# The gate's product over pairs of token blocks: seven half-size products in place of eight

## The chip, the cores and the metric

The kernel runs on one core of a Trainium2 chip. Its engines, with the names the profile gives them, are TensorE (PE, with its weight loads as PEld), VectorE (DVE), ScalarE (ACT), GpSimd (POOL) and SyncE (SP, which here issues nearly all DMAs). Each engine executes its own list of instructions in order. The metric is the device time of one execution in microseconds.

## The reference

The kernel computes one decoder layer for 2048 tokens of 1024 values, cut here to its last part, which the change concerns:

```
u    = rmsnorm(x, norm_mix)
proj = u @ w_in                          # 1024 -> 4096 columns, eight groups of 512
y    = [o_a, o_b]                        # group A: HGRN2, 4 heads; group B: stick-breaking attention, 8 heads
h    = x + y @ w_out                     # 1024 x 1024
pe   = rmsnorm(p @ w_ple_proj, ple_post_norm)           # 256 -> 1024
gate = sigmoid(rmsnorm(h, ple_gate_norm) @ w_ple_gate)  # 1024 x 1024
out  = rmsnorm(h + gate * pe, final_norm)
```

## The kernel before

**Precision.** Inputs are float32. Each matmul operand is split into a high and a low float16 part (`split`, L76 on ACT and L77 on VectorE; for weights L132 and L133), and each product is three matmuls: high by high, high by low, low by high. All of them are issued from one helper, so that every matmul of the profile has line L160.

**Stages.** Tokens are cut into 4 chunks of 512, and these into 4 blocks of 128, worked through from the last to the first. Eight groups of input weights times four chunks make 32 units; A units end in a chunked scan (`mix_A`, with seven levels, whose matmuls write `lps`, then `sp` and `op`), B units in attention. Mixed results go to `y_d` in device memory. Then follows the final stage: 16 blocks of 128 tokens. For each block `y_load` reads `y_d` into `yn`, splits it and has two DMA transposes (L697) write the left operand `fy`. `final_out` multiplies it by `w_out` (2 halves of 512 columns x 8 contraction blocks x 3 = 48 matmuls), adds `x` (L732) and takes the row's reciprocal root (L712, L83, L84); 12 matmuls make the embedding's projection, which is normalised by L740. `final_tr` splits `h` and transposes it (L748), and `final_gate` multiplies it by the gate's weights: another 48 matmuls of 128x512 into tiles named `np`. Then come the sigmoid (L762, ACT), the product (L763, GpSimd; VectorE in the last block), the sum (L764), the squares (L766), the reciprocal root, and L781 with the store of the output. In the last block the second half of the gate's product is cut into 384 and 128 columns.

**Order.** A scheduler orders the built program per engine from estimated times, so that the final stage's first blocks lie among the last mix units on every engine. Within this, `run` lets a stream of matmuls advance and steps the other tasks (`spawn`) when their time is due. Weights of the output and the gate projection are prepared by such tasks in the last input group: 24 pieces of 128x512, each a load into a ring of five `raw` buffers and two splits, into buffers that held the transposed input.

**Buffers.** Tiles rotate by tag: two buffers each of `sc`, `kq` and `y`, two each of `e0` and `e1` for `h`, three PSUM banks of the pool `ps_a` for the gate, the embedding and the mix levels (`lps`), three of `ps_pj` for the output projection, one each of `ps_o` and `ps_t`; `yn` alternates between two buffers.

## Time and profile before

| what | before |
|---|---|
| median of 3 runs | 1259.11 us (1258.26 to 1259.74) |
| the profiled execution | 1257.38 us |
| its span, first to last instruction | 1255.6 us |
| mean granted TensorE clock | 0.994 |
| PE busy | 1206.9 us, 96% of the span |
| DVE busy | 872.0 us, 69% |
| ACT busy | 596.8 us, 48% |
| POOL busy | 356.4 us, 28% |

The busy shares are means over the whole span and hide that stages differ: the tables of stretches below show that the end of the span is another regime than its start. Durations in the rows are those of one execution. An instruction's duration includes the fill and drain of its pipeline, so instructions that follow one another start closer together than they last. "xN" behind a row counts equal instructions that were put into one row, and its time runs from the first start to the last end.

### The profile page before, as it was taken

Reading aid. Unit: us, or ns where it says so; the run is one execution under the profiler, and the core shown is the slowest. Engines: PE = TensorE matmul, PEld = TensorE weight load, DVE = VectorE, ACT = ScalarE, POOL = GpSimd, SP = SyncE. Lnnn points to the kernel's source line nnn. Section 1 sums busy time; section 2 is a strip of 40 time slices with the busy share of each in tenths; the row PEclk is TensorE's granted clock in tenths of the full one; section 3 lists DMA queues with packets and bytes.
Section 4 is the critical chain, followed back from the end, with each engine's and each line's share of the span. In section 5 each row is a group of like instructions: output and inputs, shape, how many; then the busy total and the mean of one; then the engine's idle time right before and its main releaser. Section 6 shows DMA issues by size and latency. Waiting matters only on the chain.

```text
span 1255.6 us, 25850 instructions
## 1 busy us (share of the span) xinstructions
PE 1206.9 (96%) x9802; PEld 771.1 (61%) x9802; DVE 872.0 (69%) x1736; ACT 596.8 (48%) x1507; POOL 356.4 (28%) x472
## 2 busy tenths in 40 slices
PE   8887899999999999999999999898999999999997
PEld 7664666777766776677677766565544444444443
DVE  5779699976589995589997568998845344344233
ACT  7665544544454454464454445565534333333222
POOL 4248441114441212444112444110121211111212
PEclk9999999999999999999999999999999999999999
DMA  9896831156661046772126565357526636346211
GB/s 271 263 225 174 186 78 33 50 148 141 151 144 29 19 118 148 156 181 48 27 75 138 139 150 118 124 160 203 129 73 152 134 102 148 103 109 144 59 51 53
DMA packets 258469, 155.42 MB, mean 124 GB/s; under 512 B 181281, under 2 KB 226337, under 8 KB 258337
## 3 DMA queue, kind: packets, MB, share of 16 engines
...
## 4 chain that ended last, share of the span: by engine, by line
PE 69%; DVE 13%; DMA 9%; ACT 3%; issue 3%; POOL 2%; SPq 1%; POOLq 0%; DVEq 0%; ACTq 0%
PE pj L160 33%; PE np L160 28%; PE op L160 3%; PE lps L160 2%; DMA at_t<-wt_t 2%; DVE wl L133 2%; PE z L160 2%; DMA raw_t<-x_nat 2%; DVE e_t L621 1%; DMA raw_t<-w_in 1%; DMA raw_t<-w_out 1%; DVE kq_t L511 1%; ACT wh L132 1%; DVE e_t L626 1%; DMA at_t<-kp_t 1%
## 5 line engine op out<-in xcount | busy, mean ns | idle before, releaser
L160 PE MATMUL pj<-wh,xh 128*128 128x256 f16 x1024 | 280.3, 274 | 3.8 <-DVE ql_t L77 3.8
L160 PE MATMUL pj<-wl,xh 128*128 128x256 f16 x1024 | 280.4, 274 | 0.0
L160 PE MATMUL pj<-wh,xl 128*128 128x256 f16 x1024 | 280.3, 274 | 0.0
L160 PEld LDWEIGHTS <-xh 128*128 128x128 f16 x2048 | 200.4, 98 | 27.4 <-issue 0.3
L160 PE MATMUL pj<-xl,wh 128*128 128x512 f16 (+1 forms) x560 | 197.0, 361 | 2.2 <-DVE xl L260 1.7
L160 PE MATMUL pj<-xh,wh 128*128 128x512 f16 (+1 forms) x560 | 196.3, 361 | 1.6 <-DMA xh<-kq_t 1.6
L160 PE MATMUL pj<-xh,wl 128*128 128x512 f16 (+1 forms) x560 | 196.9, 361 | 0.0
L84 POOL TENSOR_TENSOR rs_y<-rs_v,mhalf 128x1 f32<-128x1 f32 (+2 forms) x87 | 77.4, 890 | 307.1 <-DVE rs_v L83 306.1
L160 PE MATMUL np<-wh,fy 128*128 128x512 f16 x512 | 155.6, 379 | 0.2 <-DVE e_t L732 0.2
L160 PEld LDWEIGHTS <-at_t 128*128 128x128 f16 x1688 | 99.2, 98 | 87.8 <-DMA at_t<-wt_t 16.7
L160 PEld LDWEIGHTS <-wh 128*128 128x128 f16 x1120 | 99.8, 98 | 85.8 <-issue 3.8
L160 PEld LDWEIGHTS <-fy 128*128 128x128 f16 x768 | 74.3, 98 | 87.8 <-issue 0.5
L160 PEld LDWEIGHTS <-xl 128*128 128x128 f16 x1024 | 100.6, 98 | 19.2 <-issue 4.2
L160 PE MATMUL np<-wh,at_t 128*128 128x512 f16 (+2 forms) x264 | 98.0, 373 | 0.9 <-ACT sc_t L762 0.9
L160 PE MATMUL np<-wl,at_t 128*128 128x512 f16 (+2 forms) x264 | 98.0, 373 | 0.0
L160 PE MATMUL np<-wh,wt_t 128*128 128x512 f16 (+2 forms) x264 | 97.9, 373 | 0.0
L160 PE MATMUL np<-wl,fy 128*128 128x512 f16 x256 | 97.0, 379 | 0.0
L621 DVE TENSOR_TENSOR_SCAN e_t<-e_t,reset 128x642 f32<-128x642 f32 x56 | 84.6, 1511 | 15.6 <-ACT e_t L616 15.5
L629 ACT CAST wt_t<-e_t 128x640 f16<-128x640 f32 (+1 forms) x64 | 44.7, 698 | 105.3 <-DVE e_t L626 90.4
L160 PEld LDWEIGHTS <-wl 128*128 128x128 f16 x560 | 53.6, 98 | 59.3 <-issue 2.5
L631 POOL TENSOR_TENSOR wt_t<-e_t,wt_t 128x512 f16<-128x512 f32 (+1 forms) x64 | 77.8, 1216 | 35.2 <-ACT wt_t L629 34.8
L76 ACT ACTIVATE qch_t<-kq_t 128x256 f16<-128x256 f32 x112 | 46.3, 414 | 77.8 <-DVE kq_t L511 53.3
...
## 6 DMA issues: line engine op xcount, KB each, us to landing
raw_t<-w_in SPq DMA_DIRECT2D x61, 256.0 KB, 3.6
raw_t<-x_nat SPq DMA_DIRECT2D x56, 256.0 KB, 3.7
y_d<-y_t SPq DMA_DIRECT2D x32, 256.0 KB, 2.5
...
out<-y_t SPq DMA_DIRECT2D x31, 256.0 KB, 2.1
...
```

Of the source, the lines that this page charges most:

```text
L76: nc.scalar.activation(hi, src, AF.Copy, scale=scale)
L84: nc.gpsimd.tensor_tensor(y, v, mhalf[:, 0:n], op=ALU.pow)
L132: nc.scalar.activation(self.h[:, k, :], self.r[k], AF.Copy, scale=g)
L133: nc.vector.scalar_tensor_tensor(self.l[:, k, :], self.r[k], g, self.h[:, k, :], op0=ALU.mult, op1=ALU.subtract)
L160: nc.tensor.matmul(out_, lhsT, rhs, start=start, stop=stop)
L511: nc.vector.tensor_tensor(act, act, other, op=ALU.mult)
L621: nc.vector.tensor_tensor_scan(fl(pr_), fl(f), fl(reset), 0.0, op0=ALU.mult, op1=ALU.max)
L626: nc.vector.tensor_tensor(sg[:, :, :w_], sg[:, :, :w_], pr_[:, :, :w_], op=ALU.mult)
L629: nc.scalar.copy(wt[:, :, :w_], sg[:, :, :w_])
L631: nc.gpsimd.tensor_tensor(wt[:, :, 3 * P : 3 * P + lw], sg[:, :, :lw], wt[:, :, :lw], op=ALU.subtract)
```

## The change

A pair of token blocks is treated as a 2 x 2 matrix: rows are the two blocks of 128 tokens (`a1?`, `a2?`), columns the two halves of the 1024 contracted values (`a?1`, `a?2`). The gate's weights are likewise four quarters of 512 x 512. Where the plain product needs eight products of quarters, the Winograd form of Strassen's scheme needs seven, each 4 contraction blocks x 3 = 12 matmuls of 128x512 (84 per pair in place of 96), of sums and differences of the quarters.

- Left operands (`pair_parts`): sums and differences of `h`, of which `a11`, `s2`, `s1`, `a12`, `s3`, `s4`, `a22` are each split and transposed (L817, twice 128x512 to 4 x 128 x 128). The row's factor is now applied before the split.
- Weights: the quarters `11` and `22` are prepared in the last input group (8 pieces in place of 16 for the gate), the combinations `t1` to `t4` and the quarter `21` by `gate_combined`, a task that is started when the final stage begins. For each of 4 contraction blocks it issues 4 loads into the `raw` ring (now six buffers), 8 ACT, 6 GpSimd and 3 VectorE instructions of 128x512.
- Results (`gate_pair`): seven products in sequence; VectorE adds PSUM tiles to running sums (L878), and each of the four results then takes the way of before (sigmoid, product, sum, square). The last result of the last pair has the full 512 columns.
- The gate of a pair is computed after the out and embedding products of the pair behind it; `h` of the four blocks of two pairs lives in `e`, `gs` and `fa` buffers. `yn` has one buffer. The embedding's product uses the banks `ps_o` and `ps_t`.
- A fallback that runs at run time only if a flag is set, and is not taken with these inputs, is rewritten to match; its part of the diff is left out.

```diff
+    gq = {}
+
+    def gate_tiles(names, pool, tags):
+
+        for part, tag in enumerate(tags):
+            t = pool.tile([P, KD, CH], F16, name="gq", tag=tag)
+            for i, n in enumerate(names):
+                gq[n, part] = t[:, 4 * i : 4 * i + 4, :]
+
+    def gate_plain(names):
+
+        for n in names:
+            r, c_ = int(n[0]) - 1, int(n[1]) - 1
+            for k in range(4):
+                g = gg[:, 4 * r + k : 4 * r + k + 1]
+                t = raw("gr")
+                nc.sync.dma_start(t, w_gate[c_][:, 4 * r + k, :])
+                yield 1.5
+                nc.scalar.activation(gq[n, 0][:, k, :], t, AF.Copy, scale=g)
+                nc.vector.scalar_tensor_tensor(gq[n, 1][:, k, :], t, g, gq[n, 0][:, k, :], op0=ALU.mult, op1=ALU.subtract)
+
+    def gate_combined():
+
+        for k in range(4):
+            g1, g2 = gg[:, k : k + 1], gg[:, 4 + k : 5 + k]
+            b = {}
+            for n in ("11", "12", "22", "21"):
+                r, c_ = int(n[0]) - 1, int(n[1]) - 1
+                b[n] = raw("gr")
+                nc.sync.dma_start(b[n], w_gate[c_][:, 4 * r + k, :])
+            yield 2.0
+            for n in ("11", "12", "22"):
+                nc.scalar.activation(b[n], b[n], AF.Copy, scale=g2 if n == "22" else g1)
+            nc.gpsimd.tensor_tensor(b["11"], b["12"], b["11"], op=ALU.subtract)
+            nc.gpsimd.tensor_tensor(b["12"], b["12"], b["22"], op=ALU.subtract)
+            nc.gpsimd.tensor_tensor(b["22"], b["22"], b["11"], op=ALU.subtract)
+            yield 2.0
+            nc.scalar.activation(gq["21", 0][:, k, :], b["21"], AF.Copy, scale=g2)
+            nc.vector.scalar_tensor_tensor(gq["21", 1][:, k, :], b["21"], g2, gq["21", 0][:, k, :], op0=ALU.mult, op1=ALU.subtract)
+            nc.vector.scalar_tensor_tensor(b["21"], b["21"], g2, b["22"], op0=ALU.mult, op1=ALU.subtract)
+            for n, t in (("t1", "11"), ("t3", "12"), ("t2", "22"), ("t4", "21")):
+                nc.scalar.copy(gq[n, 0][:, k, :], b[t])
+                (nc.vector if n == "t4" else nc.gpsimd).tensor_tensor(gq[n, 1][:, k, :], b[t], gq[n, 0][:, k, :], op=ALU.subtract)
+            yield 4.0
...
-        t = kv.tile([P, KD * CH], F16, name="yn", tag=f"bkv{n % 2}")
+        t = kv.tile([P, KD * CH], F16, name="yn", tag="bkv0")
...
+    def final_emb(st, ph, pl):
+
         pps = []
-        yield from nat_proj(ps_a, "a", ph, pl, 2, lambda half, k: (wph[:, k, hss[half]], wpl[:, k, hss[half]]), pps)
+        for half, (pool, tag) in enumerate(((ps_o, "o"), (ps_t, "t"))):
+            ps = pool.tile([P, CH], F32, name="np", tag=tag)
+            n = 0
+            for k in range(2):
+                for a, bb in ((ph(k), wph), (ph(k), wpl), (pl(k), wph)):
+                    mm(ps, a, bb[:, k, hss[half]], n == 0, n == 5)
+                    n += 1
+                yield
+            pps.append(ps)
...
+    def pair_parts(s1, s2, last):
+
+        if last:
+            t = [kv.tile([P, KD * CH], F16, name="lh", tag=tag).rearrange("p (q i k t) -> p q i k t", q=4, i=2, k=4) for tag in ("bkv0", "bkv2")]
+            slots = [[t[i // 4][:, i % 4, j] for j in range(2)] for i in range(7)]
+        else:
+            slots = []
+            for tag in ("wt", "at", "kp0", "kp1", "wt", "at"):
+                t = f16(tag, (P, 2, 4, P))
+                slots.append([t[:, 0], t[:, 1]])
+            slots.append([f16(tag, (P, 4, P)) for tag in ("vh", "vl")])
+        (a11, a12), (a21, a22), r1, r2 = s1["h"], s2["h"], s1["rn"], s2["rn"]
+
+        def put(src, r=None):
+            hi, lo = f16("qh"), f16("ql")
+            if r is None:
+                nc.scalar.copy(hi, src)
+                nc.vector.tensor_tensor(lo, src, hi, op=ALU.subtract)
+            else:
+                split(hi, lo, src, r)
+            dst = slots.pop(0)
+            for d, s in zip(dst, (hi, lo)):
+                nc.sync.dma_start(d, s, transpose=True)
+            return dst
+
+        lhs = {}
+        d21, g11 = f32("sc"), f32("sc")
+        nc.gpsimd.tensor_tensor(d21, a21, a22, op=ALU.add)
+        nc.scalar.activation(g11, a11, AF.Copy, scale=r1)
+        lhs["a11"] = put(a11, r1)
+        s2_ = f32("y")
+        nc.vector.scalar_tensor_tensor(s2_, d21, r2, g11, op0=ALU.mult, op1=ALU.subtract)
+        lhs["s2"] = put(s2_)
+        lhs["s1"] = put(d21, r2)
+        lhs["a12"] = put(a12, r1)
+        nc.vector.scalar_tensor_tensor(g11, a21, r2, g11, op0=ALU.mult, op1=ALU.subtract)
+        lhs["s3"] = put(g11)
+        nc.vector.scalar_tensor_tensor(s2_, a12, r1, s2_, op0=ALU.mult, op1=ALU.subtract)
+        lhs["s4"] = put(s2_)
+        lhs["a22"] = put(a22, r2)
+        return lhs
+
+    def gate_pair(sts, rows, lhs, last):
+
+        G = p2(-SH - SW)
+        bank = []
+        ss = [small("ssg2", 2, 4) for _ in range(2)]
+
+        def part(i, half, gt):
+
+            p_, h_ = sts[i]["pe"][half], sts[i]["h"][half]
+            nc.scalar.activation(gt, gt, AF.Sigmoid, scale=G)
+            (nc.vector if last else nc.gpsimd).tensor_tensor(p_, gt, p_, op=ALU.mult)
+            nc.vector.tensor_tensor(h_, h_, p_, op=ALU.add)
+            nc.scalar.activation(f16("kn"), h_, AF.Square, accum_out=ss[i][:, half : half + 1])
+
+        def end(i):
+            h, s_ = sts[i]["h"], small("ss1", 1)
+            nc.vector.tensor_tensor(s_, ss[i][:, 0:1], ss[i][:, 1:2], op=ALU.add)
+            rf = rsqrt(s_, 1, 1.0 / D, EPS)
+            for half in range(2):
+                gf = gfin[:, hss[half]]
+                if last and i:
+                    nc.gpsimd.tensor_tensor(h[half], h[half], gf, op=ALU.mult)
+                    if half:
+                        nc.scalar.activation(h[half], h[half], AF.Copy, scale=rf)
+                    else:
+                        nc.vector.tensor_scalar(h[half], h[half], rf, None, op0=ALU.mult)
+                else:
+                    nc.vector.scalar_tensor_tensor(h[half], h[half], rf, gf, op0=ALU.mult, op1=ALU.mult)
+                (nc.scalar if last and i and half else nc.sync).dma_start(out[rows[i], hss[half]], h[half])
+
+        def prod(left, n):
+
+            bank.append(pa("gate"))
+            for k in range(4):
+                wh_, wl_ = gq[n, 0][:, k, :], gq[n, 1][:, k, :]
+                (lh_, ll_) = lhs[left]
+                for i, (a, bb) in enumerate(((lh_, wh_), (lh_, wl_), (ll_, wh_))):
+                    mm(bank[-1], a[:, k, :], bb, k == 0 and i == 0, k == 3 and i == 2)
+                yield
+
+        def plus(dst, other):
+            nc.vector.tensor_tensor(dst, bank[-1], other, op=ALU.add)
+
+        yield from prod("a11", "11")
+        x1, u2 = f32("sc"), f32("sc")
+        nc.scalar.copy(x1, bank[-1])
+        yield from prod("s2", "t2")
+        plus(u2, x1)
+        yield from prod("s1", "t1")
+        u4, c22 = f32("y"), f32("y")
+        plus(u4, u2)
+        yield from prod("a12", "21")
+        plus(x1, x1)
+        part(0, 0, x1)
+        yield from prod("s3", "t3")
+        plus(c22, u4)
+        plus(u2, u2)
+        part(1, 1, c22)
+        yield from prod("s4", "22")
+        plus(u4, u4)
+        part(0, 1, u4)
+        end(0)
+        yield from prod("a22", "t4")
+        plus(u2, u2)
+        part(1, 0, u2)
+        end(1)
...
-        if g == 7 and i0 < 3 and c > 0:
-            w_new(9 + i0)
-            spawn(prepare_task(9 + i0), 0.5, 1)
-
-    for n in range(9, 12):
-        if n not in ws:
-            w_new(n)
-            for _ in prepare_task(n):
+        if g == 7 and i0 == 0:
+            w_new(9)
+            spawn(prepare_task(9), 0.5, 1)
+        if g == 7 and i0 == 1:
+            gate_tiles(("11", "22"), xpool, ("xh2", "xl2"))
+            spawn(gate_plain(("11", "22")), 0.5, 1)
+
+    drain(len(order) - 1)
+    gate_tiles(("21", "t1"), xpool, ("xh1", "xl1"))
+    gate_tiles(("t2", "t3"), xpool, ("xh0", "xl0"))
+    t4 = kv.tile([P, KD, CH], F16, name="gq", tag="bkv1")
+    gq["t4", 0], gq["t4", 1] = t4[:, 0:4, :], t4[:, 4:8, :]
+    spawn(gate_combined(), 1.0)
+    gpost, gfin, wph, wpl = late_weights()
+    tail = len(order)
...
+    for m in range(NB // 2):
+        for n in (2 * m, 2 * m + 1):
+            run(out_block(n), tail)
+            if m:
+                run(emb_block(n - 2), tail)
+        if m == 1:
+            drain(tail)
+        final = m == NB // 2 - 1
+        if final:
+            lhs[m] = pair_parts(sts[2 * m], sts[2 * m + 1], True)
+        if m:
+            j = 2 * m - 2
+            run(gate_pair([sts[j], sts[j + 1]], [rws[j], rws[j + 1]], lhs[m - 1], False), tail)
+        if not final:
+            lhs[m] = pair_parts(sts[2 * m], sts[2 * m + 1], False)
+    j = NB - 2
+    for n in (j, j + 1):
+        run(emb_block(n), tail)
+    run(gate_pair([sts[j], sts[j + 1]], [rws[j], rws[j + 1]], lhs[j // 2], True), tail)
```

The scheduler's order of GpSimd in the last mix A unit, before: the mix's mask product (L488) and clears, and reciprocal roots (L84). Here `sc_t` and `kp_t` are the mix's tiles.

```order
L488 TENSOR_TENSOR sc_t<-kq_t 128x512
L84 TENSOR_TENSOR rs_y<-rs_v,mhalf 128x4
L84 TENSOR_TENSOR rs_y<-rs_v,mhalf 128x1
L519 MEMSET sc_t 128x512
L487 MEMSET kp_t 128x1024
L84 TENSOR_TENSOR rs_y<-rs_v,mhalf 128x1
L84 TENSOR_TENSOR rs_y<-rs_v,mhalf 128x4
```

The same place after (L530, L561 and L529 are the former L488, L519 and L487; `raw_t` holds raw weights, `gq` the float16 parts of a combination):

```order
L530 TENSOR_TENSOR sc_t<-kq_t 128x512
L84 TENSOR_TENSOR rs_y<-rs_v,mhalf 128x4
L173 TENSOR_TENSOR raw_t<-raw_t 128x512
L174 TENSOR_TENSOR raw_t<-raw_t 128x512
L182 TENSOR_TENSOR gq<-raw_t,gq 128x512
L175 TENSOR_TENSOR raw_t<-raw_t 128x512
L182 TENSOR_TENSOR gq<-raw_t,gq 128x512
L561 MEMSET sc_t 128x512
L182 TENSOR_TENSOR gq<-raw_t,gq 128x512
L529 MEMSET kp_t 128x1024
L173 TENSOR_TENSOR raw_t<-raw_t 128x512
L84 TENSOR_TENSOR rs_y<-rs_v,mhalf 128x1
```

The six instructions of the first contraction block stand around the clear of the last mix unit's tile; 18 more of the same kinds follow, mixed with reciprocal roots, and then the addition L822 of the first pair's left operands.

SyncE's queue at the same place, before: loads of the last weights and of `x`, the store of a mix result (`y_d`), transposes.

```order
L808 DMA gw<-g_post 128x1024
L809 DMA gw<-g_fin 128x1024
L788 DMA raw_t<-p_t 128x512
L726 DMA raw_t<-x_nat 128x512 x6
L377 DMA y_d<-y_t 128x4x128
L697 DMA_TRANSPOSE fy<-yn 128x8x128 x2
L726 DMA raw_t<-x_nat 128x512
L689 DMA yn<-y_d 128x1024
```

After (L956, L957, L768, L419, L739, L596 and L731 are the former L808, L809, L726, L377, L697, L554 and L689):

```order
L956 DMA gw<-g_post 128x1024
L957 DMA gw<-g_fin 128x1024
L169 DMA raw_t<-w_gate 128x512
L419 DMA y_d<-y_t 128x4x128
L169 DMA raw_t<-w_gate 128x512 x4
L739 DMA_TRANSPOSE fy<-yn 128x8x128
L596 DMA_TRANSPOSE at_t<-kp_t 128x8x128
L169 DMA raw_t<-w_gate 128x512 x3
L739 DMA_TRANSPOSE fy<-yn 128x8x128
L768 DMA raw_t<-x_nat 128x512 x2
L731 DMA yn<-y_d 128x1024
L169 DMA raw_t<-w_gate 128x512 x3
```

The loads of the gate's weights stand between the store of `y_d`, the transposes and the `x` loads; the last of the first contraction block's four is behind the store.

## Rows read from the trace of the kernel before

**Rows 1.** Stretches: us, busy (x) of PE, PEld, DVE, ACT, POOL, PEclk, DMA share, GB/s.
```profile
850.00:900.00 50.00, 45.49 (x372) 25.95 (x370) 44.00 (x106) 26.02 (x73) 3.46 (x5) 1.00 0.65 177
900.00:950.00 50.00, 49.06 (x291) 23.88 (x290) 30.18 (x71) 20.39 (x60) 11.20 (x13) 1.00 0.44 102
950.00:1000.00 50.00, 50.00 (x233) 22.68 (x232) 21.28 (x47) 18.59 (x45) 10.65 (x13) 1.00 0.58 128
```

**Rows 2.** The chain that ended last: start us, us, what.
```profile
932.93 312.28 PE np L160 x1452
```

**Rows 3.** What TensorE waited for, 780 to 960: us in total, times, longest.
```profile
PE lps L160 <- ACT kp_t L76: 6.3, 4, 2.7
PE lps L160 <- DVE qcl_t L77: 2.4, 2, 1.4
```

**Rows 4.** Weight splits in group 7: ns min/median/max, first and last start.
```profile
L133 DVE SCALAR_TENSOR_TENSOR wl<-raw_t,gg,wh x16: 739/743/745, 809.3 to 847.7; 128x512 f16<-128x512 f32 x16
```

**Rows 5.** Timeline of the end: start us, us, engine, line, out<-in, idle before.
```profile
1246.32 0.22 PE L160 MATMUL np<-wh,wt_t 128*128 128x128 f16 x1
...
1246.58 0.37 ACT L762 ACTIVATE sc_t<-np,rs_y 128x128 f32<-128x128 f32 x1 [0.70 <-PE np L160]
1246.98 0.29 DVE L763 TENSOR_TENSOR kq_t<-sc_t,kq_t 128x128 f32<-128x128 f32 x1
...
1247.30 0.29 DVE L764 TENSOR_TENSOR e_t<-e_t,kq_t 128x128 f32<-128x128 f32 x1
...
1247.80 0.31 ACT L766 ACTIVATE kn_t<-e_t 128x128 f16<-128x128 f32 x1
```

**Rows 6.** ACT by form, 858 to 1256: xcount, busy us, mean ns, idle before.
```profile
L762 ACT ACTIVATE sc_t<-np,rs_y 128x512 f32<-128x512 f32 x31 | 21.2, 685 | 72.7 <-PE np L160 72.7
...
L766 ACT ACTIVATE kn_t<-e_t 128x512 f16<-128x512 f32 x31 | 19.5, 629 | 56.8 <-DVE e_t L764 56.4 <-DVE ss L718 0.4
```

**Rows 7.** Timeline of VectorE as the final stage begins.
```profile
862.81 1.89 DVE L77 SCALAR_TENSOR_TENSOR wp<-raw_t,wp 128x512 f16<-128x512 f32 x3
...
877.31 0.42 DVE L77 SCALAR_TENSOR_TENSOR kp_t<-kq_t,kp_t 128x256 f16<-128x256 f32 x1
...
918.83 1.26 DVE L77 SCALAR_TENSOR_TENSOR sl<-st__12449,sh 128x128 f16<-128x128 f32 x1 [0.72 <-ACT sh L76]
...
922.50 0.29 DVE L77 SCALAR_TENSOR_TENSOR sl<-st__12449,sh 128x128 f16<-128x128 f32 x1 [1.43 <-ACT sh L76]
...
940.58 1.73 DVE L77 SCALAR_TENSOR_TENSOR gs_t<-e_t,fa_t 128x512 f16<-128x512 f32 x1 [0.75 <-ACT fa_t L76]
...
955.25 1.41 DVE L740 SCALAR_TENSOR_TENSOR kq_t<-np,rs_y,gw 128x512 f32<-128x512 f32 x2 [0.73 <-POOL rs_y L84]
```

**Rows 8.** Timeline of SyncE's queue.
```profile
872.72 0.40 SPq L377 DMA_DIRECT2D y_d<-y_t  x1
...
881.01 1.24 SPq L554 DMA_TRANSPOSE at_t<-kp_t  x1
```

**Rows 9.** DMA issues: count, KB each, median us from issue to landing.
```profile
raw_t<-w_gate SPq DMA_DIRECT2D x16, 256.0 KB, 3.2
...
fy<-yn SPq DMA_TRANSPOSE x32, 3.3
```

**Rows 10.** Timeline of GpSimd.
```profile
918.67 1.27 POOL L763 TENSOR_TENSOR kq_t<-sc_t,kq_t 128x512 f32<-128x512 f32 x1 [3.98 <-ACT sc_t L762]
...
940.49 1.27 POOL L763 TENSOR_TENSOR kq_t<-sc_t,kq_t 128x512 f32<-128x512 f32 x1
...
955.18 1.27 POOL L763 TENSOR_TENSOR kq_t<-sc_t,kq_t 128x512 f32<-128x512 f32 x1
```

**Rows 11.** GpSimd by form, whole span: xcount, busy us, mean ns, idle before.
```profile
L763 POOL TENSOR_TENSOR kq_t<-sc_t,kq_t 128x512 f32<-128x512 f32 x30 | 37.9, 1264 | 127.0 <-ACT sc_t L762 127.0
...
L488 POOL TENSOR_TENSOR sc_t<-kq_t 128x512 f32<-128x512 f32 x16 | 25.8, 1611 | 89.8 <-DVE kq_t L412 89.2 <-DVE rs_v L83 0.6
```

**Rows 12.** One stretch of 10 us: columns as in Rows 1.
```profile
920.00:930.00 10.00, 10.00 (x58) 4.88 (x56) 2.97 (x10) 2.95 (x10) 1.81 (x2) 1.00 0.14 28
```

More of the change, by code (lines that the diff above doesn't have):

```diff
@@ L150, in w_new @@
         else:
[L151 to L154 removed]
+            ws[n] = Weights(w_out[1], gy, xpool, (f"xh{NC - 1}", f"xl{NC - 1}"))
     clock = [0.0]
@@ L719, in row_rsqrt, with final_out @@
         return rsqrt(s_, 1, scale, eps, post)
-    def final_out(st, yh, yl, ph, pl, rows):
+    def final_out(st, yh, yl, rows, tags=("e0", "e1")):
         xn = []
@@ L773, in final_gate @@
             ot = f32("y")
-            if last:
-                nc.gpsimd.tensor_tensor(h[half], h[half], gfin[:, hss[half]], op=ALU.mult)
-            if last and half:
-                nc.scalar.activation(ot, h[half], AF.Copy, scale=rf)
-            elif last:
-                nc.vector.tensor_scalar(ot, h[half], rf, None, op0=ALU.mult)
-            else:
-                nc.vector.scalar_tensor_tensor(ot, h[half], rf, gfin[:, hss[half]], op0=ALU.mult, op1=ALU.mult)
-            (nc.scalar if last and half else nc.sync).dma_start(out[rows, hss[half]], ot)
+            nc.vector.scalar_tensor_tensor(ot, h[half], rf, gfin[:, hss[half]], op0=ALU.mult, op1=ALU.mult)
+            nc.sync.dma_start(out[rows, hss[half]], ot)
     def p_parts(src, w):
@@ L865, in trunk_kernel @@
-    run(final_gate(*prev, last=True), -1)
-    def final_block(yh, yl, ph, pl, rows):
-        st = {}
-        for _ in final_out(st, yh, yl, ph, pl, rows):
-            pass
+        if g == 7 and i0 == 0:
[6 more added lines that the diff above has]
+    gate_tiles(("21", "t1"), xpool, ("xh1", "xl1"))
@@ L871, in final_block @@
+    j = NB - 2
+    for n in (j, j + 1):
+        run(emb_block(n), tail)
+    run(gate_pair([sts[j], sts[j + 1]], [rws[j], rws[j + 1]], lhs[j // 2], True), tail)
+    def final_block(yh, yl, ph, pl, rows):
+        st = {"post": p2(-SH - SW)}
+        for stage in (lambda: final_out(st, yh, yl, rows), lambda: final_emb(st, ph, pl)):
+            for _ in stage():
+                pass
         final_tr(st)
@@ L884, in trunk_kernel, with full_rows @@
     far = nc.values_load(fint[0:1, 0:1], min_val=0, max_val=1)
-    def full_rows(rs, gkv, gyt, cc, bb):
+    def full_rows(rs, gkv, cc, bb):
         r0 = cc * CH + bb * P
         rows = bass.ds(r0, P)
-        yh, yl = gyt[:, :, 0:P], gyt[:, :, P : 2 * P]
-        ya = f32("sc")
-        nc.sync.dma_start(ya, y_d[rows, 0 : 4 * P])
-        yp = [f16(f"kp{i}") for i in range(2)]
-        split(yp[0], yp[1], ya, p2(SY))
-        for t, p_ in zip((yh, yl), yp):
-            nc.sync.dma_start(t[:, 0:4, :], p_, transpose=True)
         nc.vector.memset(rs, 0.0)
@@ L958, in trunk_kernel @@
             with tc.For_i(0, CB, 1) as bb:
-                full_rows(rs, gkv, gyt, cc, bb)
+                full_rows(rs, gkv, cc, bb)
+        for i, tags in enumerate((("xh2", "xl2"), ("xh1", "xl1"))):
+            ws[10 + i] = Weights(w_gate[i], gg, xpool, tags)
+            ws[10 + i].prepare(range(KD))
+        with tc.For_i(0, NC, 1) as cc:
+            with tc.For_i(0, CB, 1) as bb:
+                full_out(cc, bb)
 def lay_out(x, p, norm_mix, w_in, a_out_norm, b_out_norm, w_out, lb_logits,
```

92 lines of the change are left out of this document (43 added, 49 removed).

## The prediction

> **What bounds the kernel now.** I first read the table of stretches. From 950 to 1000 us TensorE is busy for all 50.00 us at full clock, and VectorE for 21.28 [rows 1]; the four rows after it, to 1200, are alike (233 or 234 matmuls each). In that steady part time is simply a count of matmuls: 233 of 128x512 in 50.00 us, so 0.2146 us each. The chain of waits says the same of the end: 312.28 us of nothing but the line of matmuls, from 932.93 on [rows 2]. The start-up of the final stage is different: in 850 to 900 VectorE is busy for 44.00 of 50 us and TensorE for 45.49 [rows 1], and the list of what TensorE waits for names the scaled halves of the last mix A units' operands, 6.3 us for ACT's `kp_t` and 2.4 us for VectorE's `qcl_t` [rows 3]. So there are two questions: how many matmuls go, and what the change puts into a start-up in which VectorE is already nearly full.
>
> **What goes: matmuls.** A pair of blocks had 2 × 48 gate products of 128x512 and gets 7 products × 4 contraction blocks × 3 halves = 84. Eight pairs save 8 × 12 = 96 matmuls, at 0.2146 us [rows 1] 20.6 us, all of it in a stretch where TensorE is the bound. In the steady part I expect nothing to take it back. A pair took 216 matmuls, 46.4 us, and takes 204, 43.8 us. VectorE gets seven adds, three combinations and three low halves more per pair, 13 × 0.6 = 7.9 us (the 0.6 is worked out below); with 21.28 of 50 [rows 1], 19.7 of 46.4, it comes to some 27 of 43.8 us. The left operands of a pair are made a whole product stage ahead.
>
> **What goes: weight splits.** Eight of the 24 splits in the last input group are not made there: 8 VectorE instructions of 0.74 us [rows 4] (and 8 casts on ACT), 5.9 us on each, in a stretch where TensorE's two largest waits come to 8.7 us [rows 3]. Most of these waits are on the mix's own chain, so I take −1 us, bounds 0 and −2.
>
> **What comes: a longer tail.** Before, the last product is cut so that only 128 columns follow the last matmul at 1246.32: sigmoid at 1246.58, product 1246.98, sum 1247.30, square 1247.80 [rows 5]; the span ends at 1255.6, 9.1 us after the last matmul's end. Now 512 columns follow. An add to the running sum comes ahead of the sigmoid (0.69 us, as any 128x512 VectorE instruction [rows 7]); the sigmoid goes from 0.37 to 0.69 and the square from 0.31 to 0.63, the means of their full-width forms [rows 6], product and sum from 0.29 to 0.69 each. That is 0.69 + 0.32 + 0.32 + 0.40 + 0.40 = 2.1 us; I take 2.2, as two output multiplications of block 14 now stand on VectorE ahead of block 15's sum. Bounds: +1.2 (only the add and the two VectorE widths not overlapped, less a shorter gap) and +3.5 (both multiplications, 1.4, in full).
>
> **What comes: the weights' combinations, as the final stage begins.** For each of four k there are 4 loads of raw weights, 8 ACT, 6 GpSimd and 3 VectorE instructions of 128x512, and the second product (s2 by t2) needs all four. GpSimd, which is idle there now but for one-column powers and clears, gets 24 of these, and one addition for the first left operand: 25.
>
> When does it begin? The queues are in order. The last of the first k's loads stands on SP behind the store of `y_d`, which is issued at 872.72 [rows 8]; a weight load lands 3.2 us after its issue [rows 9], so about 875 to 876 us on the clock of before (I take 875), and the last mix A unit is then still running.
>
> What does it cost? In the changed order VectorE has, from that point to s2's low half, 86 instructions: 30 of 128x512 with two SBUF inputs, 8 of the same with a gain column, 12 of 256 and 4 of 128 columns, and 32 that read at most one SBUF tensor (six of 512 columns from PSUM, one masked copy of 512 and eight of 256, eight of 128, nine tiny). The rows give 0.60 us for one of the first kind when they follow one another (three in 1.89), 0.42 for 256 columns with its end, 0.34 without it [rows 7], 0.74 for the gain kind, 0.70 spaced [rows 4]: 30 × 0.605 + 8 × 0.70 + 12 × 0.336 + 4 × 0.24 = 28.7 us, and the 32 others, at the same rates, 9.7 us. Alone that would be 38.4 us, to 913.
>
> But GpSimd and VectorE get in each other's way. At 918.67 GpSimd begins a product of 1.27 us, and a 128x128 subtraction that VectorE begins at 918.83 takes 1.26 us, where the same one takes 0.29 at 922.50. At 940.49 and 940.58 it happens again: 1.73 us for a 128x512 subtraction that takes 0.69 elsewhere. At 955.18 GpSimd runs the same product and VectorE's two multiplications of a PSUM tile take 1.41 together, undisturbed [rows 7, 10]. So an instruction with two SBUF inputs waits for most of GpSimd's one; from 918.67 to about 919.8 are 1.1 us. It goes both ways: GpSimd's mask product L488, made while VectorE is busy, has a mean of 1611 ns against 1264 of the gate's [rows 11].
>
> The Trainium skill, "SBUF — State Buffer", section "Who interferes with whom", states that a VectorE instruction with two SBUF inputs contends with a GpSimd instruction that reads SBUF, that one with at most one SBUF input does not, and that the later one waits for the whole of the other. The trace agrees in all three cases (1.26, 1.73 and 1.41 us). By it the 25 instructions and VectorE's 54 two-input ones would stand in one line; without it they would overlap, which is the first rival.
>
> I take the exclusive sum: 28.7 + 25 × 1.1 = 56.2 us, and half of the 9.7 of others, which can run while GpSimd holds: 61 us. From 875 that is 936. Then s2's low part has to be transposed: SP needs 1.24 us for one transpose [rows 8] and it lands 3.3 after issue [rows 9], and there is about 1.5 us of queueing behind the transposes of other operands: the second product starts at T = 942. Below that the cost could be nearly nothing (first rival), above it loads and transposes can add (second rival). What makes this bite is TensorE's own order: the last mix A levels stand at 77, 98, 119, 134 and 159 matmuls of the final stage instead of 106 to 180, and the second gate product at 216, so it can't run ahead; the other 1416 matmuls are all behind s2.
>
> **The sum.** From T: 1416 × 0.2146 = 303.9 us; some 14 small matmuls of the mix, 0.8; the tail 9.1 + 2.2 = 11.3. The span is T + 316.0. With T = 942: 1258.0. Plus 1.5 us for the projections of pair 2's first block, whose `e` buffers wait for pair 0's outputs (before, only two blocks share them; bounds 0 and 4), less 1 for the last group: 1258.5, against 1255.6 before, +2.9. The profiled execution took 1257.38, so 1260.3; it lies 1.7 under the median of the runs, 1259.11, and on that basis I predict 1262. The saving of 20.6 us is thus spent: 2.2 in the tail and about 20 in the start-up. The turning point is T near 939.6 (1255.6 − 316.0), before the two small terms.
>
> **Rivals.**
> 1. The combinations fall into gaps (faster). GpSimd has almost nothing there, and VectorE is not full everywhere: from 920 to 930 it is busy for 2.97 of 10 us [rows 12]. If the two hide under one another, GpSimd sets the pace: 875 + 2 for ACT's scalings + 25 × 1.27 = 909; three waits for the next k's raw buffers of 3.3 us make 919, VectorE's subtraction and the transpose 6: T = 925, with a little left of the collisions 927. The span is 927 + 316 + 0.5 = 1243.5, so about 1247 on the runs' basis. It decides from T below 939: each collision that is hidden is worth 1.1 us, and three of 25 are enough for a gain. For it speaks that a VectorE row that waits for a combination anyway loses nothing to a collision; against it that VectorE was at 44.00 of 50 in 850 to 900 [rows 1], before anything was added.
> 2. Data waits on top of the collisions (slower). The raw ring has six buffers and each k needs four, shared with the `x_nat` and `p` loads; in SP's order the gate's loads stand between transposes of `fy` and those of the mix, so one that waits for a buffer holds up the transposes behind it, and a VectorE row waiting for its combination holds up the mix levels behind it. At 3.3 us of landing and one transpose of 1.24 for each of three changes of k, 13.5 us: T = 955.5, the span 1272, and 1275 on the runs' basis. For it: in before's last mix A units TensorE already waits for such rows [rows 3]. Against: part of that wait is the same time in which collisions are paid.
> 3. The steady part takes its toll. Three banks rotate through the seven products, and a product can't start until the add of the third last has run; if VectorE is late by 2 us once in each of seven pairs, 14 us go, also without trouble in the start-up: 1247 + 14 = 1261. Against it: VectorE at 27 of 43.8 us a pair, and a product lasts 2.6 us against 0.7 for an add. I give it little and count it with the forecast's upper half.
>
> **How the numbers follow.** Chances: the forecast 0.50, with a range of its own of 1255 to 1271 (T from 935 to 951); rival 1 0.33; rival 2 0.14; rival 3 0.03. A measurement of this kernel tells about 0.2% from no change, 2.5 us, so "same" is 1256.6 to 1261.6. Of the forecast's 0.50 I put 0.03 below that, 0.20 in it and 0.27 above. Faster is 0.33 + 0.03 less 0.01 = 0.35; same 0.20; slower 0.27 + 0.14 + 0.03 and the rounding 0.01 = 0.45. The range takes in rival 1 from 1244 and rival 2 up to 1275.
>
> **What would show it.** Matmuls of the final stage: 1632 at 0.2146 us, packed without gaps from the second product on, and 20.6 us less of them. GpSimd's 24 combinations with durations well above 1.27 us, or VectorE's neighbours at 1.3 to 1.7 instead of 0.6, bear out the collisions; if both are at their plain durations, rival 1 holds. The first matmul of the second product near 942 bears out the sum, near 927 rival 1, near 955 rival 2; then TensorE's waits should name `wt_t` or the combined weights, and SP's waits the raw buffers. Last matmul to the end of the span: 11.3 us instead of 9.1. The forecast is wrong if the second product begins before 937, or if TensorE waits in the steady part.

## The result and the profile after

The changed kernel takes 1302.65 us (median of 4 runs, 1300.84 to 1308.58) against 1258.68: ratio 1.0358, 95% interval 1.0336 to 1.0380. It is slower, and by far more than the forecast of 1262 and its upper end of 1275. The profiled execution took 1300.84 us, its span 1299.1, 43.5 more than before. Runs in a slower state, as one of e4 at 2115.21 us with a granted clock of 0.556, are left out of every figure below.

First the stretches, with the columns of [rows 1] (stretch, us, busy us and count of PE, PEld, DVE, ACT, POOL, PEclk, DMA share, GB/s):

```profile
850.00:900.00 50.00, 44.30 (x363) 27.05 (x363) 47.03 (x92) 31.51 (x79) 21.74 (x17) 0.93 0.56 159
900.00:950.00 50.00, 43.02 (x260) 20.71 (x258) 39.76 (x70) 25.14 (x61) 22.39 (x16) 0.93 0.68 173
950.00:1000.00 50.00, 44.93 (x199) 19.32 (x198) 34.10 (x63) 22.05 (x52) 14.10 (x15) 0.97 0.43 99
...
1150.00:1200.00 50.00, 43.27 (x193) 19.17 (x193) 28.18 (x51) 18.01 (x40) 10.52 (x11) 0.95 0.52 106
```

In the start-up VectorE and GpSimd are fuller than in [rows 1] (GpSimd 21.74 of 50 in place of 3.46), as forecast. But from 950 on TensorE is not packed: 199 and 193 matmuls in 50 us where the forecast had 233, with PEclk below 1.

How far had the final stage come at 950? Its matmuls from 840 to that time (stretch, us, PE busy and count, clock, DMA share, GB/s), first `np` of the kernel before, then `np` and `gate` of the kernel after:

```profile
840.00:950.00 110.00, 80.52 (x356) 1.00 0.60 148
```

```profile
840.00:950.00 110.00, 54.96 (x219) 0.94 0.62 164
```

```profile
840.00:950.00 110.00, 12.25 (x52) 0.94 0.62 164
```

That gives 356 of 1752 before (48 of these are the two narrow cuts of the last half-block) and 271 of 1632 after: 85 fewer, at 0.2146 us 18.2 us. From there on the kernel after has 1361 matmuls, 292.1 us if packed, which would end at 1242.1. The last one ends at 1283.5, 4.91 us after the start of the last group, so 41.4 us are lost. Before, the same sum loses 2.1. The tail from the last matmul's end is 15.5 us against 9.1.

```profile
1278.64 4.91 PE L202 MATMUL gate<-gq,lh 128*128 128x512 f16 x22
```

So the account is: start-up +18.2, matmuls saved −20.6, stalls and slow matmuls after 950 +39.3, tail +6.5: +43.4, against 43.5 measured.

The four pairs from the third to the sixth hold 33 of the 41 us. One row for each, from the first matmul of one gate to that of the next, for 204 matmuls that need 43.8 us:

```profile
1033.77:1085.30 51.53, 46.12 (x206) 20.41 (x204) 27.48 (x49) 19.10 (x42) 10.50 (x11) 0.93 0.51 118
1085.30:1135.42 50.12, 45.70 (x205) 20.27 (x204) 27.94 (x51) 18.17 (x42) 11.19 (x11) 0.97 0.54 134
1135.42:1188.10 52.68, 45.64 (x205) 20.24 (x204) 27.53 (x50) 18.71 (x41) 10.52 (x11) 0.97 0.54 110
1188.10:1241.95 53.85, 46.90 (x205) 20.59 (x204) 29.03 (x54) 21.69 (x48) 11.97 (x12) 0.90 0.51 113
```

Each has one long stall. TensorE's waits from 950 to 1262 name mainly two releasers (us, times, longest). They hold 22.9 of the 29.1 us that TensorE waits there; the kernel before has no wait at all after 950:

```profile
PE gate L202 <- ACT sc_t L882: 12.4, 2, 7.0
PE gate L202 <- DVE sc_t L878: 10.5, 3, 5.5
```

What stands behind this is seen on ACT and TensorE in the first of these pairs (start, us, engine, line, out<-in, idle before):

```profile
1037.18 0.60 ACT L759 ACTIVATE kn_t<-np 128x512 f16<-128x512 f32 x1
...
1046.09 1.15 ACT L76 ACTIVATE yn<-yn 128x512 f16<-128x512 f32 x2 [8.22 <-DMA yn<-y_d]
1047.14 0.57 ACT L882 COPY sc_t<-gate 128x512 f32<-128x512 f32 x1
```

```profile
1041.97 0.38 PE L202 MATMUL np<-wh,fy 128*128 128x512 f16 x1
1047.76 4.68 PE L202 MATMUL gate<-gq,kp_t 128*128 128x512 f16 x12 [5.41 <-ACT sc_t L882]
1052.28 2.75 PE L202 MATMUL gate<-gq,wt_t 128*128 128x512 f16 x12
```

The copy L882 frees the PSUM bank of the gate's first product, which the fourth product needs. That product ended near 1036.5. ACT is idle for 8.22 us in front of two casts of `yn`, because they wait for the load of `y`; the copy stands behind them in ACT's list and comes at 1047.14, and TensorE's fourth product starts 5.41 us late. Behind the stall 12 matmuls take 4.68 us, those of the next product 2.75. The granted clock says why. After the idle time it is 0.50, the lower of the two levels, 1.2 GHz:

```profile
1048.00:1050.00 2.00, 2.00 (x6) 0.73 (x5) 1.33 (x3) 0.00 (x0) 0.00 (x0) 0.50 0.75 145
```

In the sixth pair it is the copy again (7.0 us). In the fourth and fifth the adds L878 stand behind VectorE's low halves of `yn` in the same way (4.3 and 5.5 us). And why is `y` late? SyncE's queue in that pair:

```profile
1005.61 0.85 SPq L936 DMA_DIRECT2D raw_t<-p_t  x2
1016.99 0.34 SPq L865 DMA_DIRECT2D out<-gs_t  x1
1017.44 1.23 SPq L817 DMA_TRANSPOSE at_t<-qh_t  x1
...
1034.35 1.22 SPq L817 DMA_TRANSPOSE vl_t<-ql_t  x1
1035.66 2.64 SPq L739 DMA_TRANSPOSE fy<-yn  x2
...
1040.31 0.33 SPq L731 DMA_DIRECT2D yn<-y_d  x1
```

The queue rests from 1006.5 to 1017, since the next store waits for the end of the gate before it. Then come twelve of the pair's fourteen operand transposes, about 1.2 us each (one 1.97), up to 1035.6, and only then those of `fy`, though the halves of `yn` that they read were made by 1012.5. The load of the next `y` has to wait in the single buffer for these to land. It is issued at 1040.31 and lands at 1046, after 5.7 us, where the median load of `y` takes 3.6. TensorE doesn't need that `y` before 1072. It waits for it only because the gate's copy stands behind the casts in order.

### The profile page after: what moved, and what is told of

Its sections match the earlier page's. It is cut to its first block, busy times and chain, and to the rows that moved or that the text cites. A ratio compares the mean times of both kernels' runs of the same rounds, so it can differ in the third digit from the quotient of the medians.

```text
span 1299.1 us, 26062 instructions
## 1 busy us (share of the span) xinstructions
PE 1205.5 (93%) x9682; PEld 765.0 (59%) x9682; DVE 972.8 (75%) x1844; ACT 637.8 (49%) x1568; POOL 408.2 (31%) x502
## 4 chain that ended last, share of the span: by engine, by line
PE 53%; DVE 18%; DMA 14%; ACT 5%; issue 4%; POOL 2%; SPq 2%; DVEq 0%; POOLq 0%; ACTq 0%
PE pj L202 34%; PE np L202 7%; PE gate L202 5%; DMA yn<-y_d 4%; PE op L202 3%; DMA fy<-yn 2%; PE lps L202 2%; PE z L202 2%; DVE kq_t L553 1%; DVE wl L133 1%; DMA raw_t<-x_nat 1%; DVE e_t L663 1%; DMA raw_t<-w_in 1%; DVE kp_t L77 1%; DVE yn L77 1%
## 5 line engine op out<-in xcount | busy, mean ns | idle before, releaser
L84 POOL TENSOR_TENSOR rs_y<-rs_v,mhalf 128x1 f32<-128x1 f32 (+2 forms) x87 | 82.9, 954 | 299.1 <-DVE rs_v L83 242.1
L202 PE MATMUL np<-wh,fy 128*128 128x512 f16 x512 | 158.9, 386 | 0.0
L202 PEld LDWEIGHTS <-kp_t 128*128 128x128 f16 x1512 | 76.9, 99 | 65.7 <-issue 20.1
L663 DVE TENSOR_TENSOR_SCAN e_t<-e_t,reset 128x642 f32<-128x642 f32 x56 | 86.1, 1538 | 16.9 <-ACT e_t L658 16.6
L202 PEld LDWEIGHTS <-at_t 128*128 128x128 f16 x1328 | 65.1, 99 | 54.3 <-DMA at_t<-wt_t 16.7
L76 ACT ACTIVATE kp_t<-kq_t 128x256 f16<-128x256 f32 (+1 forms) x128 | 59.2, 463 | 36.7 <-DVE kq_t L553 23.6
L202 PE MATMUL lps<-qch_t,kp_t 128*128 128x64 f16 x896 | 65.4, 194 | 9.8 <-ACT kp_t L76 7.7
```

Of the source, the lines that this page charges most:

```text
L76: nc.scalar.activation(hi, src, AF.Copy, scale=scale)
L84: nc.gpsimd.tensor_tensor(y, v, mhalf[:, 0:n], op=ALU.pow)
L202: nc.tensor.matmul(out_, lhsT, rhs, start=start, stop=stop)
L663: nc.vector.tensor_tensor_scan(fl(pr_), fl(f), fl(reset), 0.0, op0=ALU.mult, op1=ALU.max)
```

## The experiments

The theories on the stalls of the pairs: the single `yn` buffer alone makes `y` late; or SyncE's queue does, by its order and the fourteen transposes in it, whatever the buffers; or the two together, which only runs with both changed can show. In every run the scheduler orders all queues anew, so an edit can also move instructions that it doesn't name. No run's edit moves the copy itself ahead of the casts. Beside the theories stands the forecast's own step, that VectorE and GpSimd hinder one another, against its first rival, that they hardly do (e3, e8, e10), and the tail has two runs of its own (e11, e12).

Times are medians; "done at 950" counts the final stage's matmuls as above; stalls are us of one wait of TensorE; "end" is the time from the last matmul's end to the span's end. e4 is a variant of the kernel before, which has 356 done at 950 and an end of 9.1; all others are variants of the kernel after.

| run | us | ratio to before (95%) | done at 950 | stalls over 2 us after 1030 | end |
|---|---|---|---|---|---|
| after | 1302.65 | 1.0358 (1.0336 to 1.0380) | 271 | 5.4, 4.3, 5.5, 7.0 | 15.5 |
| e1 | 1295.28 | 1.0271 (1.0236 to 1.0306) | 219 | 5.6, 4.6 | 16.5 |
| e2 | 1305.27 | 1.0349 (1.0319 to 1.0378) | 262 | 4.7, 7.1, 3.1, 5.6 | 16.8 |
| e3 | 1301.50 | 1.0331 (1.0299 to 1.0362) | 292 | 5.9, 7.3, 4.8, 7.8 | 15.3 |
| e4 | 1264.77 | 1.0029 (1.0011 to 1.0047) | 322 | none | 9.4 |
| e5 | 1286.03 | 1.0229 (1.0206 to 1.0252) | 270 | 4.0, 3.0, 4.9 | 15.4 |
| e6 | 1332.77 | 1.0577 (1.0538 to 1.0615) | 233 | 8.5, 11.0, 7.1, 6.4 | 15.5 |
| e7 | 1274.89 | 1.0128 (1.0102 to 1.0155) | 235 | none | 17.2 |
| e8 | 1291.71 | 1.0265 (1.0240 to 1.0290) | 305 | 6.0, 3.3, 4.9, 7.5 | 15.6 |
| e9 | 1270.20 | 1.0099 (1.0066 to 1.0133) | 267 | none | 16.8 |
| e10 | 1274.65 | 1.0136 (1.0096 to 1.0175) | 306 | 3.7 | 16.9 |
| e11 | 1272.13 | 1.0130 (1.0090 to 1.0171) | 306 | none | 16.7 |
| e12 | 1268.81 | 1.0078 (1.0064 to 1.0093) | 265 | 2.4 | 15.7 |

**e1, two slots for y.**

```diff
-        yf = t[:, 0 : 2 * D].bitcast(F32)
-        nc.sync.dma_start(yf, y_d[rows, :])
...
+        hl = [yt["n"][:, (n % 2 * 2 + i) * D : (n % 2 * 2 + i + 1) * D] for i in range(2)]
...
+            yf = raw("yn_f")
+            nc.sync.dma_start(yf, y_d[rows, hs])
```

> Change: y is loaded in halves into the raw ring, and the split halves alternate between two slots of the one yn tile, so a load of y no longer waits for the transposes of the block before. Theory A (late y: with one yn buffer the load waits for the transposes, and ACT's copy L882 and VectorE's adds L878 of the gate stand in order behind the casts of that y; TensorE then waits for a bank): the four stalls of 4.3 to 7.0 us at 1047, 1100, 1151 and 1203 and the half-clock matmuls after them go, a pair takes about 44 us in place of 50 to 54, total about 1265 to 1270. Theory B (SyncE's queue: the transposes of fy stand behind fourteen of the gate's operands, whatever buffer y is in): the stalls stay, total 1297 to 1303. Theory C (collisions of VectorE and GpSimd in each pair): unchanged, 1300.

In two of the four pairs the waits fell to 2.3 and 1.0 us in sum, in the other two a stall of 5.6 and one of 4.6 us stayed, and the start became worse (219). Neither theory's forecast came true alone: the buffer is one part.

**e2, stores on another queue.**

```diff
-                (nc.scalar if last and i and half else nc.sync).dma_start(out[rows[i], hss[half]], h[half])
+                (nc.scalar if last and i and half else nc.sync if last else nc.gpsimd).dma_start(out[rows[i], hss[half]], h[half])
```

> Change: the output stores of pairs 0 to 6 are issued from GpSimd's queue in place of SyncE's. Theory A (late y through the single buffer): SyncE's transposes start when their operands exist, stores before them cost little; total 1295 to 1303. Theory B (SyncE's queue is held up by stores that wait for the end of the gate before): the operands' transposes and those of fy come earlier by some us per pair, the stalls shrink by half or more, total about 1280.

No gain, but the queue wasn't freed either. SyncE now rests ahead of a load of `x`, which waits for VectorE, 14.3 us in place of 10.5 ahead of the store:

```profile
SPq L768 <- DVE gs_t L774: 14.3, 1, 14.3
```

The third pair's first combined operand is cast only at 1022.11 (1015.81 in the changed kernel), and its transpose starts at 1023.16 (1017.44). So the run shows only that the stores are not the one thing that holds the queue.

**e3, the combinations on VectorE** (the six GpSimd instructions of `gate_combined`; one is shown).

```diff
-            nc.gpsimd.tensor_tensor(b["11"], b["12"], b["11"], op=ALU.subtract)
+            nc.vector.tensor_tensor(b["11"], b["12"], b["11"], op=ALU.subtract)
```

> Change: the 24 combinations and low parts that GpSimd makes in gate_combined are made by VectorE. If the two engines exclude one another (forecast's step), 24 x 1.1 us of lock become 24 x 0.6 us of VectorE: the second product starts some 8 to 12 us earlier than 936.9, total about 1291 to 1294 with the stalls of later pairs unchanged. If GpSimd's work was hidden, VectorE gets 14.5 us more work: the second product starts 5 to 14 us later, total 1305 to 1315.

By 950 21 matmuls more are done (4.5 us), although the second product starts later (945.4), and none of it is left at the end. Neither side of the expectation came true; e8 tells more on the price.

**e4, the kernel before with one `yn` buffer.**

```diff
-        t = kv.tile([P, KD * CH], F16, name="yn", tag=f"bkv{n % 2}")
+        t = kv.tile([P, KD * CH], F16, name="yn", tag="bkv0")
```

> Change: the kernel before, with one yn buffer in place of two and nothing else. If the single buffer by itself costs (theory A in its plain form): 16 blocks, some us each, total 1275 or more. If it costs only together with the pair's order and SyncE's longer queue (theory B, or A and B together): a block there has 23 us for a chain of load 3.9, casts 2, transposes 2.6 + 3.3 us, so 1257 to 1263.

About 4 us by the ratio (interval 1.4 to 5.9). TensorE stays packed after 950, so in the plain kernel the single buffer costs only in the start-up, where the profiled execution has 34 matmuls fewer done by 950 (PEclk and counts as in [rows 1]):

```profile
950.00:1000.00 50.00, 50.00 (x233) 22.71 (x232) 22.38 (x45) 18.16 (x44) 10.48 (x12) 1.00 0.48 117
1000.00:1050.00 50.00, 50.00 (x234) 22.64 (x232) 22.51 (x46) 19.04 (x46) 9.45 (x12) 1.00 0.57 133
```

**e5, one transposing DMA per operand.**

```diff
-            hi, lo = f16("qh"), f16("ql")
+            hl = f16("qh", (P, 2, CH))
+            hi, lo = hl[:, 0], hl[:, 1]
...
+            if whole:
+                nc.sync.dma_start(whole.pop(0), hl.rearrange("p l c -> p (l c)"), transpose=True)
```

> Change: high and low half of a gate operand lie in one tile and are transposed by one DMA of 128x1024 in place of two of 128x512 (eight transposes per pair in place of fourteen; the seventh operand keeps two). A transpose takes SyncE 1.2 us whatever its size, so about 7.5 us of SyncE's queue per pair go, and the transposes of fy and the loads of y behind them come that much earlier. Theory B (SyncE's queue is what makes y late): the four stalls of 4.3 to 7.0 us vanish, about 25 to 35 us less with their half-clock matmuls, total 1268 to 1278. Theory A (only the single buffer): the stalls stay at 4 us or more, total 1295 to 1303.

16.6 us less, with the single buffer kept. The sixth pair's stall is gone; 4.0, 3.0 and 4.9 us remain in the three before it. The edit does more than shorten the queue: the high and low half now share one tile, also in the mix units, and in the scheduler's new order `fy`'s transposes stand among the operands' (in the third pair at 1024.18 and 1028.58, after at 1035.66). Which of these gave how much isn't shown; together they are worth about two fifths of the 39 us.

**e6, y's loads and transposes on ACT's queue.**

```diff
-        nc.sync.dma_start(yf, y_d[rows, :])
+        nc.scalar.dma_start(yf, y_d[rows, :])
...
-            nc.sync.dma_start(yt[n][i], hl[i], transpose=True)
+            nc.scalar.dma_start(yt[n][i], hl[i], transpose=True)
```

> Change: the loads of y and the transposes of fy are issued from ACT's queue in place of SyncE's; the single buffer stays. Theory B: y no longer stands behind the gate operands' transposes, the stalls vanish, 20 to 35 us less, unless ACT (1.25 us per transpose, four per pair) becomes the engine that the gate waits for: total 1270 to 1285. Theory A: 1295 to 1310.

The opposite of what the theory of the queue expects: 30 us slower. 38 matmuls fewer are done by 950 (233), 8.2 us; the rest is lost in the pairs. The chain of `y` now waits inside ACT's own list, and the copy still stands behind it: the transposes of `fy`, the load that waits for them, then L882, before which ACT idles another 3.52 us:

```profile
1062.28 2.82 ACTq L739 DMA_TRANSPOSE fy<-yn  x1
...
1069.74 0.34 ACTq L731 DMA_DIRECT2D yn<-y_d  x1
1070.13 0.58 ACT L882 COPY sc_t<-gate 128x512 f32<-128x512 f32 x1 [3.52 <-DMA fy<-yn]
```

So e6 is no test of SyncE's queue by itself, since it brings the issues into ACT's list. It shows that what `y` waits for hurts where it stands ahead of the gate's copy on the same engine.

**e7, the edits of e5 and e1 together.**

> Change: e5 and e1 together (one transposing DMA per operand, and two slots for y). If both the queue and the buffer count: no stall over 1 us in the pairs, TensorE packed from the third pair on, 30 to 40 us less than the changed kernel, total 1262 to 1272. If one of them is all: as the better of e1 (1295) and e5.

No stall over 2 us after 1030; 27.8 us less than the changed kernel, a little above the 1262 to 1272 expected. The rest of the distance is the worse start (235 done).

**e8, without GpSimd's combinations**: the sums are left out, and a shorter `memset` stands for the low parts.

```diff
-            nc.gpsimd.tensor_tensor(b["11"], b["12"], b["11"], op=ALU.subtract)
-            nc.gpsimd.tensor_tensor(b["12"], b["12"], b["22"], op=ALU.subtract)
-            nc.gpsimd.tensor_tensor(b["22"], b["22"], b["11"], op=ALU.subtract)
...
+                    nc.gpsimd.memset(gq[n, 1][:, k, :], 0.0)
```

> Change: leaves out GpSimd's reading work in gate_combined: the three sums per contraction block are not made (the quarters are used as they are) and the low parts of t1, t2, t3 are cleared in place of subtracted, so the gate's values are not the reference's. Loads, ACT's and VectorE's instructions stay. If collisions of GpSimd and VectorE set the start-up (forecast): the second product starts at about 920 to 927 in place of 936.9, total 1286 to 1293. If the loads and transposes set it: the second product starts at 932 to 938, total 1297 to 1303.

34 matmuls more at 950 (7.3 us), the second product at 928.0 in place of 936.9, and 10.9 us less in all. VectorE, the third busy time of a row, is no longer full (first the changed kernel, then e8):

```profile
900.00:910.00 10.00, 6.47 (x47) 3.27 (x45) 10.00 (x19) 5.86 (x19) 8.72 (x7) 0.75 0.50 155
910.00:920.00 10.00, 10.00 (x69) 4.86 (x68) 9.45 (x16) 6.71 (x16) 5.12 (x5) 0.91 0.61 161
920.00:930.00 10.00, 8.93 (x55) 4.54 (x54) 10.00 (x17) 6.15 (x12) 8.54 (x6) 1.00 0.75 192
```

```profile
900.00:910.00 10.00, 10.00 (x78) 5.16 (x75) 8.63 (x25) 8.15 (x21) 1.57 (x2) 1.00 0.65 213
910.00:920.00 10.00, 10.00 (x69) 4.79 (x68) 8.49 (x19) 4.97 (x10) 0.93 (x1) 1.00 0.96 247
920.00:930.00 10.00, 10.00 (x65) 5.14 (x64) 7.06 (x15) 3.47 (x8) 0.00 (x0) 1.00 0.92 170
```

GpSimd's combinations cost about 7 to 11 us, not the 15 that lay between the forecast and its first rival. The run takes away the collisions and the wait for GpSimd's results at once, so the collisions alone may be worth less.

**e9, e5 with two slots from block 6 on.**

```diff
+        if n < 6:
+            yf = t[:, 0 : 2 * D].bitcast(F32)
+            nc.sync.dma_start(yf, y_d[rows, :])
...
+        else:
...
+            hl = [yt["n"][:, (n % 2 * 2 + i) * D : (n % 2 * 2 + i + 1) * D] for i in range(2)]
```

> Change: e5 (one transposing DMA per operand), and y in two slots through the raw ring from block 6 on only, so that the start-up keeps its loads as in e5. If the worse start of e1 and e7 (219 and 235 matmuls of the final stage done at 950, e5 270) comes from y taking raw buffers beside the gate's weights, and the packed pairs of e7 from the two slots: about 270 done at 950 and no stall over 2 us from the third pair on, total 1264 to 1270. If the packed pairs of e7 came from its other start: stalls of 3 to 5 us as in e5, total 1282 to 1288.

As expected: 267 at 950, and from 1050 the pairs are packed, 233 or 234 matmuls in 50 us, at full clock:

```profile
1050.00:1100.00 50.00, 50.00 (x233) 22.63 (x232) 32.01 (x59) 22.79 (x50) 13.76 (x14) 1.00 0.58 132
1100.00:1150.00 50.00, 50.00 (x233) 22.70 (x232) 32.20 (x60) 21.58 (x46) 11.34 (x12) 1.00 0.59 145
1150.00:1200.00 50.00, 50.00 (x234) 22.66 (x232) 29.86 (x58) 22.11 (x49) 11.90 (x13) 1.00 0.56 130
```

The copy still stands right behind a cast of `yn` (L900 is the former L882), but `y` is there, and it runs at 1039.39 in place of 1047.14:

```profile
1038.85 0.63 ACT L76 ACTIVATE yn<-raw_t 128x512 f16<-128x512 f32 x1 [0.87 <-DMA raw_t<-y_d]
1039.39 0.57 ACT L900 COPY sc_t<-gate 128x512 f32<-128x512 f32 x1
```

TensorE still waits for it, but 1.9 us in place of 5.4. So the order costs much only where `y` is late. With both causes removed and the start kept, 32 us of the 44 are gone. What remains is the start and the tail, less the matmuls saved, and a few us of waits between 950 and 1050.

**e10, e9 with the edit of e3.**

> Change: e9, and the 24 combinations and low parts on VectorE in place of GpSimd. In e3 that gave 292 matmuls done at 950 in place of 271, but no time, since later stalls took it. If it is so (gain hidden by stalls): 15 to 20 matmuls more at 950 than e9, total 3 to 5 us less than e9. If VectorE's extra work only moves the wait: as e9.

The 3 to 5 us expected did not come: the ratios of e9 and e10, 1.0099 and 1.0136, overlap in their intervals. 39 matmuls more are done at 950 than in e9, yet 533 against 531 at 1010, since the second pair's first combined operand isn't transposed earlier:

```profile
979.26 4.07 PE L202 MATMUL gate<-gq,at_t 128*128 128x512 f16 x12 [6.22 <-DMA at_t<-qh_t]
```

**e11 and e12, the tail.** e11 (from e10) lets GpSimd and ACT do block 14's output multiplications; e12 (from e9) writes `end(0)` behind `end(1)` in the last pair.

```diff
-                if last and i:
+                if last:
...
-                    if half:
+                    if half or not i:
```

```diff
-        end(0)
+        if not last:
+            end(0)
...
+        if last:
+            end(0)
```

> Change: e10, and in the last pair the output multiplications of block 14 leave VectorE (GpSimd multiplies by the gain, ACT scales). If VectorE's queue makes the tail 15.5 us in place of 11.3 (block 14's two multiplications take 2.4 us between block 15's sum and its root): last matmul to end about 2 us shorter, total 2 us less than e10. If ACT or GpSimd then come last: same as e10.

> Change: e9, and in the last pair block 14's root and output multiplications are written behind block 15's. If what makes the tail long is VectorE's two multiplications of block 14 (2.4 us) ahead of block 15's sum and root: last matmul to the end 14 to 15 us in place of 16.9, total about 2 us less than e9. If they then end last themselves (two multiplications of 0.74 and two stores behind block 15's): about the same, 16 to 17 us.

e11: the end stays at 16.7 us against e10's 16.9, as the other branch of the expectation has it. GpSimd then comes last, with a product directly before the last reciprocal root:

```profile
1256.61 1.26 POOL L876 TENSOR_TENSOR fa_t<-fa_t,gw 128x512 f32<-128x512 f32 x1
1257.83 0.55 POOL L84 TENSOR_TENSOR rs_y<-rs_v,mhalf 128x1 f32<-128x1 f32 x1
```

e12: 15.7 us in place of 16.8, about half of what was expected. No version was found that beats the kernel before; e12 is nearest, 0.8% slower.

## Why the prediction was wrong

- **"In the steady part I expect nothing to take it back": failed, and it is the main fault,** 39 of the 44 us. With the measured T of 936.9 the forecast's own sum gives 936.9 + 316.0 + 0.5 = 1253.4; the span is 45.7 more, of which only 4.2 lie in the tail. TensorE waited there, which the forecast had named as a sign against itself. Rival 3 named the right place (a bank not freed) and had 0.03; it priced VectorE's share of busy time and gave the product's 2.6 us as slack. Busy shares of engines and of SyncE's queue don't show what stands in order ahead of the instruction that frees a bank. The change list had `yn` down to one buffer and fourteen operand transposes per pair, where the kernel before has four; the working gave neither a price in the pairs. The clock's lower level after each stall, 1.3 to 2.5 us in the first product behind it (4.68, 4.11, 4.04 and 5.28 in place of 2.75), was not in it either.
- **The start-up: right in size, in part by luck.** T = 942 meant 253 matmuls done at 950; 271 were. The second product's first matmul came at 936.87, just under the 937 that the forecast had named as a sign against itself:

```profile
936.87 0.61 PE L202 MATMUL gate<-gq,at_t 128*128 128x512 f16 x2 [1.60 <-DMA at_t<-qh_t]
```

  The loss against before is 18.2 us where "about 20" was forecast. But the forecast gave all of it to the combinations.
- **Its reason: half right.** VectorE and GpSimd exclude one another as read from [rows 7, 10]. After, GpSimd's sum begins at 880.14 and lasts 1.72, VectorE's subtraction of two SBUF tensors at 880.65 lasts 1.76; an addition that reads PSUM at 882.33 takes 0.68 beside GpSimd's next:

```profile
880.14 1.72 POOL L175 TENSOR_TENSOR raw_t<-raw_t 128x512 f32<-128x512 f32 x1
881.82 1.61 POOL L182 TENSOR_TENSOR gq<-raw_t,gq 128x512 f16<-128x512 f32 x1
```

```profile
880.65 1.76 DVE L77 SCALAR_TENSOR_TENSOR ql_t<-sc_t,qh_t 128x512 f16<-128x512 f32 x1
882.33 0.68 DVE L774 SCALAR_TENSOR_TENSOR e_t<-np,raw_t 128x512 f32<-128x512 f32 x1
```

  By e8 GpSimd's combinations are worth 7 to 11 us. For the rest there is a candidate that the working put at nothing: in e4's profiled execution the single `yn` buffer alone takes 34 matmuls, 7.3 us, from the start-up of the plain kernel. No run shows what it takes from the start-up of the changed one, nor what TensorE's granted clock of 0.93 there costs (1.00 before). e10 shows that the operands' transposes come next.
- **The matmuls saved: right.** 1632 at 0.2146 us, and packed in e9 from 1050 on.
- **The tail: mis-sized**, 15.5 in place of 11.3. Three places make up the 4.2: the last add waits 1.1 us in VectorE's list; an addition takes 1.52 beside GpSimd (+0.8); block 14's multiplications take 2.42 beside GpSimd and hold up block 15's sum (+2.3). The last of these were the "output multiplications of block 14", taken as 0.1 with a bound of 1.4. Moving them (e12) gave back only 1.1 us:

```profile
1284.66 0.68 DVE L878 TENSOR_TENSOR sc_t<-gate,sc_t 128x512 f32<-128x512 f32 x1
...
1285.33 1.52 DVE L848 TENSOR_TENSOR gs_t<-gs_t,kq_t 128x512 f32<-128x512 f32 x1
...
1289.25 2.42 DVE L864 SCALAR_TENSOR_TENSOR gs_t<-gs_t,rs_y,gw 128x512 f32<-128x512 f32 x2 [0.73 <-POOL rs_y L84]
1291.60 0.15 DVE L853 TENSOR_TENSOR ss<-ssg 128x1 f32<-128x1 f32 x1
```

```profile
1285.04 1.26 POOL L858 TENSOR_TENSOR fa_t<-fa_t,gw 128x512 f32<-128x512 f32 x1 [4.26 <-ACT kn_t L849]
...
1289.35 1.77 POOL L858 TENSOR_TENSOR fa_t<-fa_t,gw 128x512 f32<-128x512 f32 x1
1292.08 0.55 POOL L84 TENSOR_TENSOR rs_y<-rs_v,mhalf 128x1 f32<-128x1 f32 x1 [0.95 <-DVE rs_v L83]
```

- The 1.5 us for pair 2's `e` buffers and the 1 us of the last group were not isolated by any run.
